# The last layer's middle down projection as seven block products, with the order of its instructions written out

## The chip, the cores and the metric

The kernel runs on one core of a Trainium2 chip. The metric is the device time of one execution in microseconds. Before the change three runs took 1272.74, 1273.72 and 1275.20 us, the median being 1273.72 us.

The engines that matter are TensorE (PE: matmuls and transposes, with PEld for its weight loads), VectorE (DVE), ScalarE (ACT), GpSimd (POOL) and SyncE (SP). SP only issues DMA transfers, and POOL's queue issues those that accumulate into their destination. Each engine runs its own instructions in a fixed order and waits on semaphores for the others.

## What is computed

The reference is a trunk of two decoder layers on 512 tokens of width 1024. Each layer has a mixer (sparse attention, gated linear attention and spatial gating) and then a feed-forward part:

```python
for l in range(DEPTH):                       # DEPTH = 2
    ...
    x = x + jnp.concatenate([o_nsa, o_gla, o_sg], axis=-1) @ w_out[l]
    h = rmsnorm(x, ffn_norm[l])
    x = x + (jax.nn.silu(h @ w_gate[l]) * (h @ w_up[l])) @ w_down[l]
return rmsnorm(x, final_norm)
```

`w_gate` and `w_up` have 1024 rows and D_FF = 2816 columns (22 tiles of 128); `w_down` is 2816 x 1024. The change concerns `@ w_down[l]` in the last layer, for 8 of the 22 tiles of its inner dimension. Everything is float32.

## The kernel before

**Precision.** An operand is kept as two tiles, `hi` (rounded to the type that TensorE takes) and `lo` (the rest). `mm3` (L384) issues three matmuls for each product: hi x hi, hi x lo, lo x hi. For weights, `w_split` (L363) makes the pair from a loaded tile `raw` of 128 x 1024: ScalarE writes `hi` (L367) and VectorE subtracts (L370). For operands, `split_psum` (L347) does the same (L348, L349). The pairs of weights live in four buffers `hl`, so that a split waits until the matmuls that used the buffer two products earlier are done. Loaded weights live in three buffers `raw`, two `wx` and two `wy`.

**The feed-forward part** (`ffn`, L1457) cuts the 22 tiles of D_FF into two halves of 11 and works in three blocks (`PARTS`): tiles 0 to 2, 3 to 6 and 7 to 10 of each half. The middle block, the one that matters here, so has 8 tiles: 4 of half 0 and 4 of half 1.

Gate and up projections of the second and third block are done by `quads` (L1519), a form of Strassen's product. It takes the operands as 2 x 2 blocks (two halves of the inner dimension, two halves of the tokens or columns) and does seven block products in place of eight, in the order 1, 2, 5, 6, 7, 3, 4. Each block product is 2 token tiles x 4 inner tiles x 3 = 24 matmuls of 512 columns. The operand sums are made ahead (`Ops`, L557). The weight sums are made in `wx` and `raw`: `summed` loads one block with SP and then adds another with a transfer that accumulates, issued on POOL's queue (L1526); for products 6 and 4, VectorE adds a block that was loaded into another buffer (L1585, L1612). The sums of results form in the PSUM banks A, B and C (two banks each), and VectorE and ScalarE take them out (`copy`, `use`).

**The down projection of a block** follows its gate and up projections. `turned` (L1654) transposes the block's result `zb` (tokens on partitions; in the last layer `zb` is the buffer `xT`) into PSUM, 16 transposes for each half, and splits it into operand tiles `act`. `down_tok` (L1381) then multiplies plainly: for each of 2 column halves, 2 pairs of token tiles, 8 inner tiles and 2 tiles of a pair, one `mm3`, which is 192 matmuls; VectorE adds the results to the residual `xt` (L1402).

In the loop over blocks (L1689) the middle block of the last layer runs as follows: gate products, up products, transposes of half 1, gate product 1 of the third block, transposes of half 0, gate product 2 of the third block, `down_tok`, and then the rest of the third block. `finish` ends the kernel.

**The order of the work.** A scheduler orders each engine's instructions by priority (`tc.high_priority`). In one part of the kernel the order is written out: `in_order` (L618) takes the instructions that were traced since `mark[0]`, numbers them for each engine from 0 in the order of tracing, leaves out the DMA transfers, and chains them in the order of the table `ORDER`. Around the middle block's down projection there is no such table before the change.

Of the kernel before, what the change touches and what calls it, by code (L numbers as in the profile page):

```python
# [19 lines left out]
P = 128  # L20
# [16 lines left out]
WPRI = 400  # L37
WU = (5, 2, 1)
EPRI = 600
EP = {}  # L40
JS = 3
XPOOL = (1,)
# [61 lines left out]
    "Pool": (  # L104
        "0-2 11 20 4 3 5-6 9 7-8 10 13 19 12 14 16 15 17 38 29 18 22 21 23-24 26 25 27 47 28 33 31 30 32 56 34 36 35 37 "
        "39-42 44 46 43 45 51 49 48 50 52 55 54 53 58 57 60 59 64 61-63 65 68 66-67 71 70 72 69 73-79 "
    ),
}
LEVELS = (64, 32, 16, 8, 4, 2, 1)
# [81 lines left out]
def trunk_kernel(ctx: ExitStack, tc: tile.TileContext, a, out):  # L191
# [192 lines left out]
    def mm3(ps, lh, ll, rh, rl, start, stop, skip=False):  # L384
        nc.tensor.matmul(ps, lh, rh, start=start, stop=False, skip_group_check=skip)  # L385
        nc.tensor.matmul(ps, lh, rl, start=False, stop=False, skip_group_check=skip)  # L386
        return nc.tensor.matmul(ps, ll, rh, start=False, stop=stop, skip_group_check=skip)  # L387
# [227 lines left out]

    mark = [None]

    def in_order():  # L618
        traced = nc.cur_bb.bb.instructions
        k0 = next(k for k in reversed(range(len(traced))) if traced[k] is mark[0]) + 1  # L620
        for engine, runs in ORDER.items():
            work = [i for i in traced[k0:] if i.engine == getattr(mybir.EngineType, engine)
                    and not isinstance(i, mybir.InstDMACopy)]
            runs = [[int(n) for n in r.split("-")] for r in runs.split()]
            line = [work[n] for r in runs for n in range(r[0], r[-1] + 1)]
            assert len(set(i.name for i in line)) == len(work)
# [830 lines left out]
    def ffn(l, fp, norm, kts, ops, kts_next, nrm_next, g_next):  # L1457
# [19 lines left out]
        def plain_block(fl):  # L1477

            acts, rb = [], None
            steps = [5, 6, 7, 0]  # L1480

            def through(pss):
                gx, th, ux = t_(), t_(), t_()
                nc.vector.tensor_tensor(gx, pss[0], rb, op=ALU.mult)  # L1484
                nc.scalar.activation(th, gx, AF.Tanh, scale=0.5)
                nc.vector.scalar_tensor_tensor(ux, pss[1], 0.5, rb, op0=ALU.mult, op1=ALU.mult)
                nc.vector.tensor_tensor(ux, ux, gx, op=ALU.mult)
                nc.vector.scalar_tensor_tensor(ux, th, 1.0, ux, op0=ALU.add, op1=ALU.mult)
                act = fp.tile([P, 2, SEQ], F32R, tag="act", name=nm("act"), bufs=8)
                split_psum(act[:, 0, :], act[:, 1, :], ux)  # L1490
                acts.append(act)
            for n, f in enumerate(fl):
                pss, us = [], []
                for mat, tag in (("w_gate", "g"), ("w_up", "s")):
                    u = w_rows(a[mat][l], 0, 8, f * P, P)
                    pss.append(psum(tag))
                    us.append(u)

                ks = [(b, k) for k_ in ((range(6), (6, 7)) if n == 0 else (range(KT),)) for b in range(2) for k in k_]
                if n == 1:  # L1500
                    ks.insert(KT, None)
                for bk in ks:
                    if bk is None:
                        in_order()
                        rb = begin()
                        through(*held)
                        continue
                    b, k = bk
                    x_ = kts[k // 2]
                    ins = mm3(pss[b], us[b][:, 0, k, :], us[b][:, 1, k, :], x_[:, k % 2, 0, :], x_[:, k % 2, 1, :], k == 0, k == KT - 1)  # L1510
                if n:
                    through(pss)
                else:
                    held = [pss]
                if n and steps:
                    ops.need(steps.pop(0))
            return acts

        def quads(mat, c0, w, copy, use, pri=WPRI):  # L1519

            def rows(k0, half, u):
                return a[mat][l][(k0 + 2 * u) * P : (k0 + 2 * u + 2) * P, half * HF + c0 : half * HF + c0 + w].rearrange(
                    "(k p) c -> p k c", p=P)

            def load(dst, k0, half, u, q=None):
                (q or nc.sync).dma_start(dst[:, 0 : 2 * w].rearrange("p (k c) -> p k c", k=2), rows(k0, half, u),  # L1526
# [28 lines left out]
            def product(i, us, ps, start, stop):  # L1555
                for tt in range(2):
                    tk = slice(tt * P, (tt + 1) * P)
                    for kt in range(4):
                        u = us[kt // 2][:, :, kt % 2, :]
                        mm3(ps[tt][:, 0:w], ops.at(i, kt, 0)[:, tk], ops.at(i, kt, 1)[:, tk], u[:, 0], u[:, 1],  # L1560
                            start and kt == 0, stop and kt == 3, True)

            A = [psum("g") for _ in range(2)]

            product(1, plain(0, 0), A, True, True)
            yield
            B = [psum("s") for _ in range(2)]
            product(2, plain(4, 0), B, True, True)
            yield
            with tc.high_priority(offset=EPRI):  # L1570
                c11 = [copy(tt, 0, A[tt][:, 0:w]) for tt in range(2)]
                for tt in range(2):
                    use(tt, 0, c11[tt], B[tt][:, 0:w])
            C = [psum(x) for x in "so"]

            X, us = summed(0, 0, 0, 1, "wx")
            product(5, us, C, True, True)
# [3 lines left out]
            for u in range(2):  # L1581
                raw = raw_("wy", 2)
                load(raw, 4, 1, u)
                with tc.high_priority(offset=pri):
                    nc.vector.tensor_tensor(X[u][:, 0 : 2 * w], X[u][:, 0 : 2 * w], raw[:, 0 : 2 * w], op=ALU.add)  # L1585
                Y.append(raw)
                us.append(view(w_split(2 * w, X[u], pri)))
            product(6, us, A, False, True)
# [17 lines left out]

            us = []
            for u in range(2):
                raw = raw_("raw", 3)
                load(raw, 4, 0, u)  # L1610
                with tc.high_priority(offset=pri):
                    nc.vector.tensor_tensor(X[u][:, 0 : 2 * w], X[u][:, 0 : 2 * w], raw[:, 0 : 2 * w], op=ALU.add)  # L1612
# [41 lines left out]
        def turned(n, half):  # L1654
# [8 lines left out]
                res.append(act)  # L1663
            return res

        def down_m(fl, acts, m, nb, w, last=True, early=False):
# [22 lines left out]
        for n, (f0, nb) in enumerate(parts):  # L1689
# [3 lines left out]
            if n == 0:  # L1693
                acts = plain_block(fl)
                if xt is not None:
                    token_major(xt)
                ops.need(3)
            else:
                list(todo[n][0])
                list(todo[n][1])  # L1700
                after = last_cast[0]
# [66 lines left out]
```

## Time and profile before

The profiled execution is a fourth one, with its own time.

| | |
|---|---|
| median of three runs | 1273.72 us (1272.74 to 1275.20) |
| profiled execution | 1269.01 us |
| its span, first to last instruction | 1267.2 us |
| mean granted TensorE clock | 0.998 |
| TensorE busy | 1245.8 us (98%) |
| VectorE busy | 900.2 us (71%) |
| ScalarE busy | 662.5 us (52%) |
| middle block, last layer: up products | 1050.0 to 1088.1 us of the span |
| transposes and two gate products of the third block | 1088.1 to 1102.5 us |
| `down_tok` of the middle block | 1102.5 to 1146.0 us |

Times are counted from the start of the span. A row of the timeline has the start in us, the duration in us, the engine, the line of the kernel and the operation; `[0.56 <-ACT act L348]` behind it says how long the engine was idle just before and what ended the idle time. A row of the groups has line, engine, operation, out<-in with shapes and a count, then busy us and the mean ns of one, then the idle time before them with its releasers. A row of the windows has, for one stretch, each engine's busy time and number of instructions, then the granted clock, the mean busy share of the 16 DMA engines and GB/s. Matmuls are pipelined, so their durations overlap; what one costs is read from start to start.

### The profile page before, as it was taken

The numbers are of one execution on the slowest core, as the hardware profiler recorded it, in microseconds if no ns is written. First come the engines' busy times: TensorE is split into PE (matmuls) and PEld (weight loads), VectorE is DVE, ScalarE is ACT, GpSimd is POOL, SyncE is SP. The second block draws the span as 40 slices with busy tenths as digits, with TensorE's granted clock in tenths as the row PEclk, the third lists the DMA queues.
The fourth block names the chain that finished last, engine by engine and source line by source line (L and its number), as shares of the span: only waits on it lengthen the run. The fifth ranks groups of instructions, "written<-read, shape, count | busy, mean of one in ns | idle before, by whom it ended". The sixth has DMA issues, their size and how long they took to land.

```text
span 1267.2 us, 18084 instructions
## 1 busy us (share of the span) xinstructions
PE 1245.8 (98%) x6678; PEld 1036.3 (82%) x6678; DVE 900.2 (71%) x1549; ACT 662.5 (52%) x1256; POOL 205.3 (16%) x253
## 2 busy tenths in 40 slices
PE   8999999999999999999999999999999999999997
PEld 7887778888888888888888877788888888888886
DVE  6767789967856874587446667998776467727775
ACT  6675358865433552354346733778554345515532
POOL 0101224532000100010301002345300001000002
PEclk9999999999999999999999999999999999999999
DMA  6461350053335885483434316301433548744811
GB/s 234 132 194 34 98 128 18 19 132 117 96 107 147 197 244 131 110 212 90 114 94 152 117 34 142 97 21 48 121 115 100 132 125 228 203 110 143 222 67 67
DMA packets 134204, 155.02 MB, mean 122 GB/s; under 512 B 9306, under 2 KB 86884, under 8 KB 134116
## 3 DMA queue, kind: packets, MB, share of 16 engines
q1 hardware_dynamic: 117392, 128.81, 33.4%
q0 software_dynamic: 10208, 20.84, 9.4%
q10 hardware_dynamic: 6516, 4.22, 1.4%
q8 instruction: 52, 0.85, 0.3%
q14 instruction: 36, 0.29, 0.1%
HBM read 149.92 MB, written 2.10 MB: 120 GB/s over the span
## 4 chain that ended last, share of the span: by engine, by line
PE 85%; DVE 6%; ACT 4%; issue 2%; DMA 2%; ACTq 0%
PE banks L385 23%; PE banks L386 22%; PE banks L387 22%; PE banks L1319 3%; PE banks L1337 2%; PE banks L1336 2%; DMA raw<-in_w_in_dram 1%; ACT hl L367 1%; PE banks L1300 1%; PE banks L1301 1%; PE banks L1660 1%; PE banks L520 1%; PE banks L1033 1%; DVE hl L370 1%; DVE w1h L807 1%
## 5 line engine op out<-in xcount | busy, mean ns | idle before, releaser
L367 ACT CAST hl<-raw 128x1024 fp32r<-128x1024 f32 (+3 forms) x170 | 175.3, 1035 | 213.7 <-PE banks L387 163.4
L370 DVE TENSOR_TENSOR hl<-raw,hl 128x1024 fp32r<-128x1024 f32 (+3 forms) x170 | 204.4, 1207 | 85.5 <-ACT hl L367 84.1
L385 PE MATMUL banks<-hl,kt 128*128 128x512 f32 (+2 forms) x688 | 259.3, 377 | 1.5 <-ACT hl L367 1.4
L387 PE MATMUL banks<-hl,kt 128*128 128x512 f32 (+2 forms) x688 | 257.7, 375 | 0.0
L386 PE MATMUL banks<-hl,kt 128*128 128x512 f32 (+2 forms) x688 | 256.7, 373 | 0.0
L386 PE MATMUL banks<-kt,hl 128*128 128x512 f32 x384 | 150.1, 393 | 0.0
L385 PE MATMUL banks<-kt,hl 128*128 128x512 f32 x384 | 150.0, 398 | 0.0
L385 PEld LDWEIGHTS banks<-hl,kt 128*128 128x128 f32 x688 | 129.6, 188 | 24.6 <-ACT hl L367 2.0
L387 PE MATMUL banks<-kt,hl 128*128 128x512 f32 x384 | 149.7, 393 | 0.0
L387 PEld LDWEIGHTS banks<-hl,kt 128*128 128x128 f32 x688 | 129.8, 189 | 21.3
L386 PEld LDWEIGHTS banks<-hl,kt 128*128 128x128 f32 x688 | 129.5, 188 | 21.2
L1312 POOL TENSOR_SCALAR P<-P,rc,gates 128x384 f32<-128x384 f32 (+3 forms) x128 | 77.6, 620 | 92.5 <-DVE rc L1310 81.2
L367 ACT CAST hl<-wx 128x1024 fp32r<-128x1024 f32 x48 | 50.5, 1052 | 78.8 <-PE banks L387 72.4
L387 PEld LDWEIGHTS banks<-kt,hl 128*128 128x128 f32 x384 | 72.3, 188 | 13.7
L385 PEld LDWEIGHTS banks<-kt,hl 128*128 128x128 f32 x384 | 71.9, 188 | 14.2 <-DVE ft L1484 0.4
L386 PEld LDWEIGHTS banks<-kt,hl 128*128 128x128 f32 x384 | 72.3, 188 | 13.0
L549 DVE TENSOR_TENSOR xT<-xT,banks 128x512 f32<-128x512 f32 x56 | 37.6, 682 | 50.3 <-PE banks L387 50.1
L370 DVE TENSOR_TENSOR hl<-wx,hl 128x1024 fp32r<-128x1024 f32 x48 | 58.7, 1223 | 19.9 <-ACT hl L367 19.3
L386 PE MATMUL banks<-act,hl 128*128 128x512 f32 x172 | 67.1, 390 | 0.0
L387 PE MATMUL banks<-act,hl 128*128 128x512 f32 x172 | 67.0, 389 | 0.0
L385 PE MATMUL banks<-act,hl 128*128 128x512 f32 x172 | 66.9, 390 | 0.0
L386 PE MATMUL banks<-hl,act 128*128 128x512 f32 (+1 forms) x164 | 63.0, 384 | 0.0
(357 smaller groups left out, 2392.2 us busy)
## 6 DMA issues: line engine op xcount, KB each, us to landing
raw<-in_w_gate_dram SPq DMA_DIRECT2D x44, 512.0 KB, 3.7
raw<-in_w_up_dram SPq DMA_DIRECT2D x44, 512.0 KB, 4.3
raw<-in_w_in_dram SPq DMA_DIRECT2D x32, 512.0 KB, 3.6
raw<-in_w_down_dram SPq DMA_DIRECT2D x36, 256.0 KB, 4.0
raw<-in_w_down_dram SPq DMA_DIRECT2D x18, 512.0 KB, 3.6
raw<-in_w_out_dram SPq DMA_DIRECT2D x16, 512.0 KB, 3.4
raw<-in_cmp_w_k_dram SPq DMA_DIRECT2D x8, 512.0 KB, 3.8
raw<-in_cmp_w_v_dram SPq DMA_DIRECT2D x8, 512.0 KB, 4.4
```

The costliest lines, as they stand in the source:

```text
L367: last_cast[:] = [nc.scalar.copy(hl[:, 0, 0:n], raw[:, 0:n])]
L370: e_.tensor_tensor(hl[:, 1, 0:n], raw[:, 0:n], hl[:, 0, 0:n].bitcast(F32), op=ALU.subtract)
L385: nc.tensor.matmul(ps, lh, rh, start=start, stop=False, skip_group_check=skip)
L386: nc.tensor.matmul(ps, lh, rl, start=False, stop=False, skip_group_check=skip)
L387: return nc.tensor.matmul(ps, ll, rh, start=False, stop=stop, skip_group_check=skip)
L520: ins = nc.tensor.matmul(pw[t], xkt[n][:, kk, p, t * P : t * P + P], eu[n][0][:, q, kk, :], start=n == 0 and p + q + kk == 0, stop=n == 3 ...
L549: nc.vector.tensor_tensor(xT[:, m, :], xT[:, m, :], ps, op=ALU.add)
L807: nc.vector.tensor_tensor(hl[:, 1], raw[:, q * 512 : q * 512 + 512], hl[:, 0].bitcast(F32), op=ALU.subtract)
L1312: nc.gpsimd.tensor_scalar(ps_[i], ps_[i], rc[:, i : i + 1], gates[:, i, 3 * h + 1 + br : 3 * h + 2 + br], op0=ALU.mult, op1=ALU.mult)
L1319: nc.tensor.transpose(T[:, c : c + P], ps_[i][:, j * P : (j + 1) * P], ident)
L1336: nc.tensor.matmul(O[:, j * P : SEQ], lhs, pt[:, 0, c : c + n], start=first, stop=False)
L1337: nc.tensor.matmul(O[:, j * P : SEQ], lhs, pt[:, 1, c : c + n], start=False, stop=h > 0 and br == 1 and j == 0)
```

## The change

The last layer's middle down projection is done by `quads` too. The operands come from the transposes: `DownOps.turned(1)` transposes half 1, splits its first 256 tokens and copies all of it back to `zb`; `turned(0)` transposes half 0, splits all of it, and `sums` makes the differences and sums for products 5, 6 and 3 from the PSUM banks and the copy. `split(6)`, `split(7)` and `split(3)` make the remaining operand pairs between the products. Some of them overwrite operand tiles whose product is done. With `far=True`, `quads` adds weights for products 6 and 4 by accumulating transfers on POOL's queue and not on VectorE. Each result bank is added to the residual or subtracted from it (`add`), 14 times in place of 8.

Gate product 1 of the third block stays between the two sets of transposes; its gate product 2 now comes after the down products. The new table `ORDER_DOWN` chains 392 instructions of TensorE, 102 of VectorE and 64 of ScalarE, traced from the start of the middle block's up products to the end of its down products.

In the table's numbers, TensorE's 0 to 167 are the up products (24 each, in the order 1, 2, 5, 6, 7, 3, 4), 168 to 183 the transposes of half 1, 184 to 207 gate product 1 of the third block, 208 to 223 the transposes of half 0, and 224 to 391 the seven down products in the same order: 224 is product 1, 248 product 2, 272 product 5, 296 product 6, 320 product 7, 344 product 3, 368 product 4. Within a product the first 12 belong to the first token tile. VectorE's 30 and 31 are the last of up, 32 to 35 the splits of half 1, 38 to 41 those of half 0, 42 to 53 the sums, 54 to 57 the splits for product 5, and from 58 on the down products' weight splits (58, 59 for product 1; 64, 65 for 2; 78, 79 for 5; 84, 85 for 6; 88, 89 for 7; 94, 95 for 3; 98, 99 for 4), operand splits and additions (74 to 77, 86, 87, 90 to 93, 96, 97, 100, 101).

The core of the diff:

```diff
+OPRI = 260
...
+ORDER_DOWN = {
+    "PE": (
+        "0-1 24 2 36 3 25-27 37 28 4-5 12-15 6 16 7 38-39 8 17-21 9 40 22 48 10 41 60 29 11 61 42 49 23 30 62-64 50 "
...
+        "127-129 146-147 130 135 148 136 131 137-138 212 139-141 149-150 168 142-143 172 158-159 151 160-161 180 "
+        "152-155 181 176 216 169 162-163 182 173 170 164 184 177 174 171 165 178 217 166-167 183 175 185 179 218 213 "
+        "186-188 196-197 189-191 198 192 219 199 208 214 209 215 210-211 200 224 193 236 225 237 201 238 194 202 195 "
+        "203 226 239 204-205 220 227 221 206-207 240-242 228-229 243 230 244-245 231 222 248 232-235 246-247 249 260 "
+        "223 272 250 273 261-263 274 264-265 275 266 276 251 277-278 252-256 284 257 285 279 286 267-268 287 269-270 "
+        "288-290 258 271 259 291 280-281 296 282 292 308 297 309-310 298 311-313 299-301 293 314 294 302-304 315 "
+        "305-307 316-317 283 295 318-329 332 330 333-336 331 337-347 368 348-349 369 350 370-372 351 373 380 374 "
+        "381-382 356-357 383 358-361 352-353 375 384 362-363 354 376 364 385 365 377 366-367 355 386-391 378-379 "
+    ),
+    "DVE": (
+        "0 2 1 8 3 10 9 11-13 26 6 14-15 7 4 20-21 5 16 27 18 28 19 17 29 22-25 36 30 37 32 31 35 34 33 58-59 38-40 42 "
+        "45 48 46-47 43-44 64 49 78 50 54 65 79 55 41 56 51-53 61 66 68 75 62 70 72 60 74 63 67 84 80 69 57 73 77 85 81 "
+        "88 71 86 89 87 94 83 95 90-91 98-99 92-93 76 82 97 96 101 100 "
+    ),
+    "Activation": (
...
-    def in_order():
+    def in_order(table):
...
-        for engine, runs in ORDER.items():
+        for engine, runs in table.items():
...
-                        in_order()
+                        in_order(ORDER)
...
-        def quads(mat, c0, w, copy, use, pri=WPRI):
+        def quads(mat, c0, w, copy, use, pri=WPRI, rows=None, at=None, tags=("gg", "ss", "so"), far=False):
...
+            def grow(x, raw, half, u):
+                if far:
+                    load(x, 4, half, u, nc.gpsimd)
+                    return
+                with tc.high_priority(offset=pri):
+                    nc.vector.tensor_tensor(x[:, 0 : 2 * w], x[:, 0 : 2 * w], raw[:, 0 : 2 * w], op=ALU.add)
...
+        class DownOps:
...
+            def turned(self, half):
+                pss = []
+                for b in range(4):
+                    ps = psum(("osss", "tsto")[half][b])
+                    for t in range(NT):
+                        nc.tensor.transpose(ps[:, t * P : (t + 1) * P], zb[:, 2 * t + half, b * P : (b + 1) * P], ident)
+                    pss.append(ps)
+                for b, ps in enumerate(pss):
+                    act = fp.tile([P, 2, SEQ], F32R, tag="act", name=nm("act"), bufs=8)
+                    (self.k1 if half else self.k2).append(act)
+                    if half:
+                        split_psum(act[:, 0, 0:256], act[:, 1, 0:256], ps[:, 0:256])
+                        nc.scalar.copy(zb[:, 2 * b + 1, :], ps)
+                    else:
+                        split_psum(act[:, 0, :], act[:, 1, :], ps)
+                if not half:
+                    self.sums(pss)
...
+            def sums(self, pss):
+                tt, stt = nc.vector.tensor_tensor, nc.vector.scalar_tensor_tensor
+                s5 = []
+                for b, ps in enumerate(pss):
+                    a11, a21, s6, s3 = self.parts(b)
+                    z = t_()[:, 0:256]
+                    tt(z, ps[:, 256:512], a21, op=ALU.subtract)
+                    stt(s6, z, -1.0, a11, op0=ALU.mult, op1=ALU.subtract)
+                    stt(s3, s6, -1.0, ps[:, 0:256], op0=ALU.mult, op1=ALU.subtract)
+                    s5.append(z)
+                with tc.high_priority(offset=OPRI):
+                    for b, z in enumerate(s5):
+                        split_psum(self.at(5, b, 0), self.at(5, b, 1), z)
...
+            def add(self, t, half, *parts):
+                y = xt[:, t, half * 512 : (half + 1) * 512]
+                nc.vector.tensor_tensor(y, y, parts[-1], op=ALU.subtract if half else ALU.add)
+
+            def products(self):
+                return quads("w_down", 0, 512, self.add, self.add, rows=self.rows, at=self.at, tags=("tt", "os", "ss"), far=True)
...
                 list(todo[n][0])
+                if xt is not None and not last:
+                    mark[0] = nc.cur_bb.bb.instructions[-1]
                 list(todo[n][1])
+                if xt is not None and not last:
+                    down = DownOps(f0)
+                    down.turned(1)
+                    next(todo[n + 1][0])
+                    with tc.high_priority(offset=WPRI - OPRI):
+                        down.turned(0)
+                    g = down.products()
+                    next(g)
+                    with tc.high_priority(offset=OPRI):
+                        down.split(6)
...
+                    list(g)
+                    in_order(ORDER_DOWN)
+                    continue
```

More of the change, by code (lines that the diff above doesn't have):

```diff
@@ L106 @@
         "39-42 44 46 43 45 51 49 48 50 52 55 54 53 58 57 60 59 64 61-63 65 68 66-67 71 70 72 69 73-79 "
+    ),
+}
+ORDER_DOWN = {
[12 rows of a table added]
+    ),
+    "DVE": (
[3 rows of a table added]
+    ),
+    "Activation": (
+        "0-3 6 4 7-8 5 9 12-13 10 16 11 17 14 18 15 19 28-29 20 38 22 24 26 21 27 39 25 30 23 31-32 44 34-35 45 50 40 "
+        "36 51 42 41 33 47 37 52-53 46 43 56 49 55 57 48 54 58-63 "
     ),
@@ L1517, in plain_block, with gate_rows @@
             return acts
-        def quads(mat, c0, w, copy, use, pri=WPRI):
-            def rows(k0, half, u):
+        def quads(mat, c0, w, copy, use, pri=WPRI, rows=None, at=None, tags=("gg", "ss", "so"), far=False):
+            def gate_rows(k0, half, u):
                 return a[mat][l][(k0 + 2 * u) * P : (k0 + 2 * u + 2) * P, half * HF + c0 : half * HF + c0 + w].rearrange(
                     "(k p) c -> p k c", p=P)
+            rows, at = rows or gate_rows, at or ops.at
             def load(dst, k0, half, u, q=None):
@@ L1559, in product @@
                         u = us[kt // 2][:, :, kt % 2, :]
-                        mm3(ps[tt][:, 0:w], ops.at(i, kt, 0)[:, tk], ops.at(i, kt, 1)[:, tk], u[:, 0], u[:, 1],
+                        mm3(ps[tt][:, 0:w], at(i, kt, 0)[:, tk], at(i, kt, 1)[:, tk], u[:, 0], u[:, 1],
                             start and kt == 0, stop and kt == 3, True)
-            A = [psum("g") for _ in range(2)]
+            def grow(x, raw, half, u):
[4 more added lines that the diff above has]
+                    nc.vector.tensor_tensor(x[:, 0 : 2 * w], x[:, 0 : 2 * w], raw[:, 0 : 2 * w], op=ALU.add)
+            A = [psum(x) for x in tags[0]]
             product(1, plain(0, 0), A, True, True)
             yield
-            B = [psum("s") for _ in range(2)]
+            B = [psum(x) for x in tags[1]]
             product(2, plain(4, 0), B, True, True)
@@ L1573, in quads @@
                     use(tt, 0, c11[tt], B[tt][:, 0:w])
-            C = [psum(x) for x in "so"]
+            C = [psum(x) for x in tags[2]]
             X, us = summed(0, 0, 0, 1, "wx")
@@ L1583, in quads @@
                 load(raw, 4, 1, u)
-                with tc.high_priority(offset=pri):
-                    nc.vector.tensor_tensor(X[u][:, 0 : 2 * w], X[u][:, 0 : 2 * w], raw[:, 0 : 2 * w], op=ALU.add)
+                grow(X[u], raw, 1, u)
                 Y.append(raw)
@@ L1608, in quads @@
             for u in range(2):
[L1609 to L1612, printed above, removed]
+                raw = raw_("raw", 3) if not far else None
+                if not far:
+                    load(raw, 4, 0, u)
+                grow(X[u], raw, 0, u)
                 us.append(view(w_split(2 * w, X[u], pri)))
@@ L1664, in turned, with __init__, at, rows @@
             return res
+        class DownOps:
+            def __init__(self, f0):
+                self.f0 = f0
+                self.k1, self.k2 = [], []
+                self.op5 = fp.tile([P, 4, 2, 256], F32R, name=nm("op5"))
+            def at(self, i, kt, s_):
+                if i == 5:
+                    return self.op5[:, kt, s_, :]
+                c = 256 if i in (4, 7) else 0
+                return (self.k1 if i in (1, 6, 7) else self.k2)[kt][:, s_, c : c + 256]
+            def rows(self, k0, half, u):
+                r0 = (self.f0 + 2 * u + (0 if k0 else NF // 2)) * P
+                return a["w_down"][l][r0 : r0 + 2 * P, half * 512 : (half + 1) * 512].rearrange("(k p) c -> p k c", p=P)
+            def turned(self, half):
[15 more added lines that the diff above has]
+                    self.sums(pss)
+            def parts(self, b):
+                return [zb[:, 2 * b + h, c : c + 256] for h in (1, 0) for c in (0, 256)]
+            def sums(self, pss):
[11 more added lines that the diff above has]
+                        split_psum(self.at(5, b, 0), self.at(5, b, 1), z)
+            def split(self, i):
+                for b in range(4):
+                    a11, a21, s6, s3 = self.parts(b)
+                    if i == 7:
+                        s3 = t_()[:, 0:256]
+                        nc.vector.tensor_tensor(s3, a11, a21, op=ALU.subtract)
+                    split_psum(self.at(i, b, 0), self.at(i, b, 1), s6 if i == 6 else s3)
+            def add(self, t, half, *parts):
[3 more added lines that the diff above has]
+                return quads("w_down", 0, 512, self.add, self.add, rows=self.rows, at=self.at, tags=("tt", "os", "ss"), far=True)
@@ L1699, in ffn @@
                 list(todo[n][0])
+                if xt is not None and not last:
+                    mark[0] = nc.cur_bb.bb.instructions[-1]
                 list(todo[n][1])
+                if xt is not None and not last:
[8 more added lines that the diff above has]
+                        down.split(6)
+                    next(g)
+                    with tc.high_priority(offset=OPRI):
+                        down.split(7)
+                    next(g)
+                    with tc.high_priority(offset=OPRI):
+                        down.split(3)
+                    list(g)
+                    in_order(ORDER_DOWN)
+                    continue
                 after = last_cast[0]
```

2 rows, old and new, of the table ORDER_DOWN are left out of this document.

## The prediction

> **What bounds the kernel now.** I read the page's engine shares, then the windows around the change, then TensorE's timeline.
>
> ```profile
> span 1267.2 us, 18084 instructions
> ...
> PE 1245.8 (98%) x6678; PEld 1036.3 (82%) x6678; DVE 900.2 (71%) x1549; ACT 662.5 (52%) x1256; POOL 205.3 (16%) x253
> ```
>
> ```profile
> core 0: us, PE busy (x) PEld busy (x) DVE busy (x) ACT busy (x) POOL busy (x), PEclk, DMA share, GB/s
> 1050.00:1088.10 38.10, 38.10 (x169) 31.51 (x169) 30.65 (x33) 18.65 (x21) 4.81 (x4) 1.00 0.86 223
> 1088.10:1102.50 14.40, 14.40 (x81) 12.45 (x80) 11.24 (x15) 9.02 (x15) 0.00 (x0) 1.00 0.84 249
> 1102.50:1146.00 43.50, 43.50 (x193) 36.02 (x193) 18.68 (x21) 9.72 (x10) 2.41 (x2) 1.00 0.39 97
> ```
>
> The rows are the middle block's up products, then its transposes beside the first two gate products of the next block, then its down projection. TensorE is busy in every microsecond of all three, at full clock (column PEclk). So a matmul taken out here shortens the kernel, and there is no idle time that a new order could win: the list can only lose. The third row is the one that changes: VectorE has 24.8 us to spare in it, and DMA runs at 0.39.
>
> **The matmuls removed.** The plain product has 8 operand tiles x 4 token tiles x 2 column halves x 3 = 192 matmuls. Seven block products have 7 x 2 x 4 x 3 = 168. All are of the same shape.
>
> ```profile
> 1102.55 0.39 PE L385 MATMUL banks<-hl,act 128*128 128x512 f32 x1
> ...
> 1146.07 0.39 PE L385 MATMUL banks<-hl,kt 128*128 128x512 f32 x1
> ```
>
> These are the first start of the plain product and the first start behind it: 43.52 us for 192, so 0.2267 us each (0.39 is the pipelined length). 24 fewer are 5.44 us less. The Trainium skill ("TensorE: Matmul & The Clock Gate", Part 1) gives N / 2.4 GHz + 2.5 ns from start to start at full clock. For 512 columns that is 0.2157 us, an estimate by which the saving would be 5.18 us; the trace's cadence decides.
>
> **The transposes.** Their number stays 32. Before they stand in two blocks of 16; in the list they stand in 16 groups among matmuls.
>
> ```profile
> 1088.14 1.91 PE L1660 MATMUL banks<-ident,xT 128*128 128x128 f32 x16
> 1089.80 0.48 PE L385 MATMUL banks<-hl,kt 128*128 128x512 f32 x1
> 1090.12 0.40 PE L386 MATMUL banks<-hl,kt 128*128 128x512 f32 x1
> ```
>
> ```profile
> 822.08 0.39 PE L1348 MATMUL banks<-pcT,vcb 128*128 128x512 f32 x1
> 822.31 0.27 PE L1319 MATMUL banks<-ident,P 128*128 128x128 f32 x1
> 822.34 0.47 PE L386 MATMUL banks<-kt,hl 128*128 128x512 f32 x1
> 822.65 0.39 PE L387 MATMUL banks<-kt,hl 128*128 128x512 f32 x1
> ```
>
> A block of 16 costs 1.66 us and a first gap that is 0.32 instead of 0.23, so 0.110 each. A lone one between 512-column matmuls costs 822.65 - 822.08 - 2 x 0.2267 = 0.117. For 32 that is 0.2 us more.
>
> **What VectorE and ScalarE get.** The prices:
>
> ```profile
> L370 DVE TENSOR_TENSOR hl<-raw,hl 128x1024 fp32r<-128x1024 f32 x10 | 12.2, 1224 | 9.1 <-ACT hl L367 9.1
> L367 ACT CAST hl<-raw 128x1024 fp32r<-128x1024 f32 x10 | 10.4, 1050 | 22.6 <-PE banks L387 20.1 <-DMA raw<-in_w_gate_dram 1.7 <-DMA raw<-in_w_down_dram 0.8
> L349 DVE TENSOR_TENSOR act<-banks,act 128x512 fp32r<-128x512 f32 x8 | 5.0, 682 | 0.0
> L1402 DVE TENSOR_TENSOR zb<-zb,banks 128x512 f32<-128x512 f32 x7 | 4.8, 685 | 15.1 <-PE banks L387 15.1
> ```
>
> ```profile
> 1063.79 1.22 DVE L370 TENSOR_TENSOR hl<-wx,hl 128x1024 fp32r<-128x1024 f32 x1
> 1064.92 1.22 DVE L1612 TENSOR_TENSOR wx<-wx,raw 128x1024 f32<-128x1024 f32 x1
> ...
> 1083.76 0.68 DVE L1648 TENSOR_TENSOR ft<-ft,banks 128x512 f32<-128x512 f32 x1
> 1084.36 1.22 DVE L370 TENSOR_TENSOR hl<-raw,hl 128x1024 fp32r<-128x1024 f32 x1
> ```
>
> ```profile
> 972.23 1.43 DVE L584 SCALAR_TENSOR_TENSOR kt<-sg,kt 128x256 fp32r<-128x256 f32 x4
> ```
>
> Back to back, an operation of 1024 columns takes 1.13 us of VectorE, one of 512 takes 0.60, and one of 256 takes (1.43 - 0.08) / 4 = 0.34, where 0.08 is the overlap that the starts above show (0.68 against 0.60). Before, the down part has 8 weight splits, 8 operand splits of 512 and 8 additions: 8 x (1.13 + 0.60 + 0.60) = 18.6 us. After, it has 14 weight splits, 14 additions of 512, 4 operand splits of 512 and 36 operations of 256 (4 splits of half 1, 12 sums, 12 splits for products 5, 6, 3, and 8 for product 7): 15.8 + 8.4 + 2.4 + 12.2 = 38.8 us. VectorE gets 20 us more, in 38.1 us of products and about 9 us of transposes and gate product ahead of them. It just fits, without much to hide a mistake in the order. ScalarE's work in the stretch (14 weight casts of 1.05 and 28 shorter ones) stays below VectorE's.
>
> **What moves.** Gate product 2 of the next block goes from ahead of the down products to behind them, with its two loads on SP's queue, its splits, and the evacuations that follow it. It then stands as in the middle block, whose gate products ran so:
>
> ```profile
> 984.00:1022.00 38.00, 38.00 (x170) 31.46 (x169) 18.75 (x21) 10.92 (x12) 2.39 (x2) 1.00 0.46 111
> ```
>
> No gap, so I cost the move at nothing; the down products 3 and 4 cover its loads and splits (its weight buffers come free 23 and 8 matmuls before the list's end, 5.2 and 1.8 us, against 2.4 needed, and the second is used 6 matmuls later). The up products are only interleaved anew; the walk below finds no wait among them.
>
> **Where the list makes TensorE wait.** I laid the three lists side by side with these prices and looked for matmuls with too few others between them and what they need. When a matmul frees a weight buffer, the drain (0.39 - 0.23 = 0.16), the cast (1.05) and the subtraction (1.22) follow, 2.43 us, before the second matmul on the new weights.
>
> - Matmul 295, the last of product 5, frees the buffer that 327 in product 7 needs. Nine matmuls lie between, 2.04 us: a wait of 0.4, with the slow restart 0.5.
> - From 295 to 344 (product 3, which needs the bank that addition 91 frees) lie 26 matmuls, 5.9 us, and the wait above. VectorE has after 295 the chain of 2.4 us and then 87, 94, 83, 95, 90, 91, that is 0.60 + 1.13 + 0.34 + 1.13 + 0.60 + 0.68 = 4.5. A wait of 0.5.
> - From the end of the up products (167) to 284 (product 5, whose bank the last of the sums, 53, frees) lie 70 matmuls and 16 transposes, 17.6 us. VectorE has 25 operations from 58 to 53: 6 x 1.13 + 4 x 0.60 + 15 x 0.34 = 14.3, from about 2.0 behind 167 (operations 31, 35, 34, 33 stand first), with 0.7 of waiting for transposes that the list puts late and about 1.0 where sums follow each other through their results. That is 18.0, so 0.5 with the restart.
>
> Together 1.5 us. They are bounded by 0 (each rests on a few tenths, and a VectorE that is 3% quicker closes two) and by twice as much.
>
> **The two DMA chains.** Products 5, 6, 7 and 4 get their weights' sums by accumulating transfers on Pool's queue; 6 and 4 used VectorE for it in the gate blocks. The buffer wx is read by the split for 5, then written by the transfer, then split for 6.
>
> ```profile
> L1526 SPq DMA_DIRECT2D wx<-in_w_gate_dram x8: 367/368/411, 260.8 to 1080.3; - x8
> ...
> DMA to landing us min/median/max: 3.5/3.8/4.9
> ```
>
> ```profile
> L1526 POOL DMA_DIRECT2D wx<-in_w_gate_dram x8: 1194/1203/1642, 267.1 to 1085.4; - x8
> ...
> DMA to landing us min/median/max: 5.8/8.3/9.8
> ```
>
> The first answer is wx's plain loads, the second its accumulating ones. Matmul 229 frees the buffer for product 5's first split; from there to 296, the first of product 6, lie 53 matmuls and 2 transposes, 12.2 us. The chain needs 2.4, half a microsecond of VectorE's queue, the transfer and one cast of 1.05: 4.0 + 8.3 = 12.3 at the median. The waits above push 296 back by 0.5, so at 8.3 nothing is lost, and from 8.7 on each microsecond costs one.
>
> The second chain is new behind the change: wx is held until product 4's split, and the next gate block's product 5 needs it 78 matmuls after 337 (54 of the list and 24 of gate product 2), 17.7 us. Drain, cast, VectorE's queue (2.0), subtraction, issue (0.37), load (3.8), accumulation (8.3) and cast make 17.9, the second buffer about 1 us later with 1.4 of matmuls in between. A wait of 0.2 at the median, 1.3 at 9.8. Before, the last of these transfers started at 1080.3 and 1085.4 (the rows above), far ahead.
>
> The Trainium skill ("DMA: Bandwidth & Descriptors", the anatomy of a SWDGE transfer) fits 2.0 us + bytes / 436e3 for a transfer from GpSimd. For 512 KB that is 3.2 us, an estimate. By it both chains close 5 us early and their 0.2 us goes. The landings of 5.8 to 9.8 in this trace speak against it.
>
> **The sum.** -5.44 + 0.2 + 1.5 + 0.2 = -3.5, and half a microsecond more for restarts and for Pool's and SP's queues, whose order the list leaves out: -3.0 us. The profiled execution took 1269.01 us (span 1267.2), 4.7 below the median of the three runs, 1273.72; the difference applies to either. Forecast 1273.72 - 3.0 = **1270.7 us**. A measurement of this kernel tells 0.2%, 2.5 us, from no change.
>
> **The rivals.**
>
> *All waits hidden.* VectorE's sums come out a little quicker, transfers land at their median: -5.44 + 0.2 + 0.5 = -4.7, 1269.0 us. For it: the three waits are tenths. Against: with 38.8 us of work in some 47, VectorE can't make up a late start.
>
> *The accumulating transfers land at the top of their spread, 9.8 us.* Then 296 waits 1.1, the gate product 1.3, each with a restart and a second wait for the subtraction of about 0.3, on top of 1.5 + 0.2: a loss of 4.7, so -0.7, 1273.0 us. For it: the down stage moves 14 loads of 512 KB and 4 more for the accumulations into X in 38 us, 9.4 MB or 248 GB/s, the rate of the second window, where the DMA engines are at 0.84. Against: the up stage ran at 223 GB/s and 0.86 without one wait on TensorE.
>
> *The transfers saturate: slower than before.* The same two chains with landings of 12 us. 296 waits 3.3, the gate product 3.5, product 4 (its chain has 3 us of slack) 1.3, and 2 us of restarts and the small waits: a loss of 10, so +4.6, 1278.3 us. It decides from a landing of about 10 us on and passes +2.5 at 11. For it: 18 transfers where the plain product had 8. Against: none of the 16 accumulating wx transfers took over 9.8.
>
> **Chances.** Forecast 0.38, all hidden 0.16, top of the spread 0.34, saturated 0.12. The first two are faster by over 0.2%, the third is within, the last slower. The range goes from all hidden, less 1 us for the runs' own scatter (1272.74 to 1275.2), to the third case plus 2.5: 1268.0 to 1275.5. It leaves out the saturated case and little else.
>
> **What would show it.** Right: 168 matmuls in the down part at 0.227 us; TensorE's gaps of 0.3 to 0.7 us at product 5's second token tile, product 7's third operand and product 3's start, put down to VectorE; VectorE busy over 85% from the first sum to product 3. Wrong: gaps over 1 us ahead of product 6 or of the next block's gate product 5, put down to ScalarE behind a DMA (second and third rival); landings of wx over 9.8; a cadence other than 0.227; or new waits at the end of the kernel, which I take as unchanged.

## The result and the profile after

The change made the kernel slower. Seven executions took 1277.15 to 1280.83 us, median 1279.07, against 1268.60 to 1275.20, median 1271.04, for seven of the kernel before: a ratio of 1.0062, with a 95% interval of 1.005 to 1.0074. The forecast was 3.0 us faster, with a range from 5.7 us faster to 1.8 us slower. The loss is 8.0 us.

The profiled execution took 1278.19 us. The engines' row of its page and the windows around the change (us from:to and length, busy time and number of instructions of each engine, granted clock, DMA share, GB/s) are these. Lines of the kernel carry higher numbers than before: L385 is now L410, L367 is L392, L370 is L395, and a load (L1526) is L1553.

```profile
PE 1246.7 (98%) x6654; PEld 1031.9 (81%) x6654; DVE 920.1 (72%) x1593; ACT 674.8 (53%) x1282; POOL 215.6 (17%) x261
```

```profile
core 0: us, PE busy (x) PEld busy (x) DVE busy (x) ACT busy (x) POOL busy (x), PEclk, DMA share, GB/s
...
1102.50:1141.00 38.50, 34.58 (x145) 26.11 (x144) 29.54 (x48) 17.78 (x29) 8.48 (x7) 1.00 0.92 204
...
1147.90:1151.20 3.30, 0.25 (x2) 0.05 (x1) 0.07 (x1) 1.04 (x1) 0.00 (x0) 1.00 1.11 201
1151.20:1156.00 4.80, 4.04 (x9) 2.60 (x10) 4.03 (x5) 1.67 (x2) 0.00 (x0) 0.65 0.77 140
```

24 matmuls fewer, and yet TensorE's total has not fallen: 1246.7 us against 1245.8. A part of the reason is that matmuls at the lower clock are busy for longer (0.63 us instead of 0.39, in the rows below). In the first of these windows, the down part, it stands still for 3.9 of 38.5 us; from 1147.9 to 1151.2 it does next to nothing; and after that it runs at a granted clock of 0.65. Before, it was busy throughout, at 1.00. The share of the DMA engines went from 0.39 to 0.92 while the rate only went from 97 to 204 GB/s.

The waits of TensorE between 1090 and 1180 us, grouped (total, times, longest), say who was late. There was not one such row before.

```profile
PE banks L410 <- ACT hl L392: 5.9, 3, 3.0
PE banks L411 <- DVE hl L395: 1.6, 3, 0.8
PE banks L410 <- DVE xT L1745: 0.7, 2, 0.5
```

The last row is the forecast's wait of product 5 for the sums. The first two are the split of weights, the cast and then the subtraction. TensorE's timeline shows where: at product 6 of the down projection (1116.37) and at product 5 of the third block's gate (1151.15), where it restarts slowly.

```profile
1114.16 0.39 PE L410 MATMUL banks<-hl,op 128*128 128x512 f32 x1
1116.37 0.50 PE L410 MATMUL banks<-hl,act 128*128 128x512 f32 x1 [1.82 <-ACT hl L392]
...
1147.72 0.39 PE L412 MATMUL banks<-hl,kt 128*128 128x512 f32 x1
1151.15 0.50 PE L410 MATMUL banks<-hl,kt 128*128 128x512 f32 x1 [3.05 <-ACT hl L392]
1152.41 0.62 PE L411 MATMUL banks<-hl,kt 128*128 128x512 f32 x1 [0.76 <-DVE hl L395]
1152.83 0.63 PE L412 MATMUL banks<-hl,kt 128*128 128x512 f32 x1
...
1156.02 0.42 PE L410 MATMUL banks<-hl,kt 128*128 128x512 f32 x1
```

From 1152.41 to 1156.02 the matmuls start 0.42 us apart and more, where the rest of the stage has 0.227: eight steps take 3.61 us in place of 1.81.

The cast was itself waiting. Between 1107 and 1153 us the chain that ended last goes through three transfers: the second accumulation for product 6, the load into the first buffer of the gate's product 5, and the accumulation into its second buffer (the one into the first was issued at 1142.36):

```profile
1107.74 12.59 DMA wx<-in_w_down_dram
...
1132.52 9.21 DMA wx<-in_w_gate_dram
1141.80 0.54 issue
...
1143.61 8.93 DMA wx<-in_w_gate_dram
```

And POOL's queue shows in which order the accumulations were issued: `raw` is product 7's, `wx` is product 6's.

```profile
1102.72 1.20 POOL L1553 DMA_DIRECT2D raw<-in_w_down_dram  x1 [11.74 <-DVE xT L1744]
1104.79 1.20 POOL L1553 DMA_DIRECT2D wx<-in_w_down_dram  x1 [0.87 <-DVE xT L1745]
1106.64 1.22 POOL L1553 DMA_DIRECT2D raw<-in_w_down_dram  x1 [0.65 <-issue]
1107.74 1.38 POOL L1553 DMA_DIRECT2D wx<-in_w_down_dram  x1
```

Product 7 comes after product 6, but its accumulations go ahead of product 6's and between them, so that four are in flight at once. Product 6's land 10.4 us (1104.79 to the cast's start at 1115.27) and 12.6 us after their issue; the forecast took 8.3.

### The profile page after: what moved, and what is told of

Its sections match the earlier page's. It is cut to its first block, busy times and chain, and to the rows that moved or that the text cites. A ratio compares the mean times of both kernels' runs of the same rounds, so it can differ in the third digit from the quotient of the medians.

```text
span 1276.4 us, 18142 instructions
## 1 busy us (share of the span) xinstructions
PE 1246.7 (98%) x6654; PEld 1031.9 (81%) x6654; DVE 920.1 (72%) x1593; ACT 674.8 (53%) x1282; POOL 215.6 (17%) x261
## 4 chain that ended last, share of the span: by engine, by line
PE 78%; DVE 7%; DMA 5%; ACT 5%; issue 3%; ACTq 0%; POOL 0%; POOLq 0%; DVEq 0%
PE banks L410 21%; PE banks L411 20%; PE banks L412 20%; PE banks L1344 3%; PE banks L1362 2%; ACT hl L392 2%; PE banks L1361 2%; DVE hl L395 2%; DMA wx<-in_w_gate_dram 1%; DMA raw<-in_w_in_dram 1%; DMA raw<-in_w_down_dram 1%; PE banks L1325 1%; DMA wx<-in_w_down_dram 1%; PE banks L545 1%; PE banks L1326 1%
## 5 line engine op out<-in xcount | busy, mean ns | idle before, releaser
L392 ACT CAST hl<-raw 128x1024 fp32r<-128x1024 f32 (+3 forms) x168 | 173.0, 1034 | 193.5 <-PE banks L412 146.4
L410 PE MATMUL banks<-hl,kt 128*128 128x512 f32 (+2 forms) x688 | 259.1, 378 | 4.5 <-ACT hl L392 4.2
L395 DVE TENSOR_TENSOR hl<-raw,hl 128x1024 fp32r<-128x1024 f32 (+3 forms) x168 | 201.9, 1206 | 74.8 <-ACT hl L392 73.6
L410 PEld LDWEIGHTS banks<-hl,kt 128*128 128x128 f32 x688 | 130.0, 189 | 28.4 <-ACT hl L392 5.4
L410 PE MATMUL banks<-kt,hl 128*128 128x512 f32 x384 | 149.9, 398 | 0.0
L392 ACT CAST hl<-wx 128x1024 fp32r<-128x1024 f32 x54 | 56.8, 1051 | 89.4 <-PE banks L412 59.6
L395 DVE TENSOR_TENSOR hl<-wx,hl 128x1024 fp32r<-128x1024 f32 x54 | 66.0, 1223 | 34.6 <-ACT hl L392 34.3
L410 PEld LDWEIGHTS banks<-kt,hl 128*128 128x128 f32 x384 | 71.9, 188 | 14.1 <-DVE ft L1509 0.4
L410 PE MATMUL banks<-act,hl 128*128 128x512 f32 x172 | 66.8, 390 | 0.0
L374 DVE TENSOR_TENSOR PT<-banks,PT 128x384 fp32r<-128x384 f32 (+1 forms) x96 | 55.7, 593 | 8.5 <-ACT PT L373 8.0
```

The lines of the kernel that those rows point to most:

```text
L374: nc.vector.tensor_tensor(lo, src, hi.bitcast(F32), op=ALU.subtract)
L392: last_cast[:] = [nc.scalar.copy(hl[:, 0, 0:n], raw[:, 0:n])]
L395: e_.tensor_tensor(hl[:, 1, 0:n], raw[:, 0:n], hl[:, 0, 0:n].bitcast(F32), op=ALU.subtract)
```

## The experiments

Theory A says that the loss sits in the two transfer chains: product 6's, made late by the order on POOL's queue, and the gate product 5's, which starts only when product 4 lets `wx` go; a clock drop follows the second. Rival B says that the transfers are simply too many for the DMA engines. Rival C blames the written-out list. Eight kernels were run, in two groups (e1 to e4, e5 to e8), each group beside the kernel before on the same chip. What one kernel gains on the change, or on a kernel of the other group, is a difference of two such ratios, and uncertain by some 2 us.

| kernel | ratio to the kernel before | interval |
|---|---|---|
| the change | 1.0062 | 1.0050 to 1.0074 |
| e1: own buffers for the gate's product 5 | 1.0026 | 1.0015 to 1.0037 |
| e2: product 7's accumulations behind 6's | 1.0025 | 1.0014 to 1.0037 |
| e3: both | 1.0003 | 0.9995 to 1.0012 |
| e4: no list | 1.0100 | 1.0085 to 1.0116 |
| e5: e3, with the up transfers behind the gate's | 0.9989 | 0.9979 to 1.0000 |
| e6: 16 more matmuls in the gap | 1.0052 | 1.0040 to 1.0065 |
| e7: product 7's accumulations left out | 1.0021 | 1.0012 to 1.0031 |
| e8: kernel before, 24 matmuls left out | 0.9958 | 0.9946 to 0.9970 |

**e8, the matmuls by themselves.** In the kernel before, `down_tok` skips one of its eight operand tiles:

```diff
+                    if len(acts) < 8 or k != 3:
                         mm3(ps[b], acts[k][:, 0, tk], ...
```

> The kernel before with 24 of the 192 matmuls of the middle block's down projection left out (three of every 24, one operand tile of eight) and nothing else changed, so that the product is not complete. It measures the term on which the forecast rests, by itself: 24 x 0.2267 = 5.4 us less, a ratio of 0.9957. A rival by which the time of a matmul taken out here comes back as a wait later (for the third block's weights, or at the end) gives 0.998 to 1.000.

The ratio is 0.9958, 5.3 us of 1271. The first start of the plain product and the first start behind it, in the kernel with 168 matmuls:

```profile
1103.56 0.39 PE L385 MATMUL banks<-hl,act 128*128 128x512 f32 x1
...
1141.64 0.39 PE L385 MATMUL banks<-hl,kt 128*128 128x512 f32 x1
```

That is 38.08 us, 0.2267 each, and 5.44 less than the 43.52 of before. The saving is real and nothing takes it back, as long as nothing else changes. So whatever the change lost came with what it added.

**e4, no list.**

```diff
-                    in_order(ORDER_DOWN)
```

> The changed kernel with the list of the down stage taken out, so that the engines keep the order in which the program was scheduled; the seven products and the summed operands stay. Theory A (the loss comes from the transfer chains, not from the list's order): the transposes and the sums now stand in blocks that TensorE has to wait for, the transfer waits stay, so slower than the changed kernel by 3 us or more (1.009 or above). Rival C (the list is at fault: it puts small waits on a VectorE without room and pulls the weights' chain late): as fast as the changed kernel or faster, 1.003 to 1.006.

1.0100, so the list is worth 0.4% and rival C falls. The longest waits of TensorE from 1085 to 1180 us without it:

```profile
PE banks L410 <- ACT hl L392: 5.1, 2, 4.0
PE banks L410 <- DVE xT L1745: 2.9, 2, 2.0
PE banks L1721 <- ACT xT L1728: 1.5, 1, 1.5
```

The waits for the weights' split stay (5.1 against 5.9), and waits for the sums and for transposes' banks come on top. Part of the 0.4% is the clock: behind waits of 2.04 and 3.99 us this kernel runs at half cadence (last section). The list does its work; it does not reach the transfers.

**e2, the order on POOL's queue.** An edge puts product 7's accumulations behind the last one that product 6 needs:

```diff
-                    load(x, 4, half, u, nc.gpsimd)
+                    grown[:] = [load(x, 4, half, u, nc.gpsimd)]
...
-                    load(raw, k1, half1, u, nc.gpsimd)
+                    with tc.issue_after(grown[0].ins) if grown else ExitStack():
+                        load(raw, k1, half1, u, nc.gpsimd)
```

> The changed kernel, but on Pool's queue the accumulations for product 7 are issued behind the two for product 6 instead of ahead of them and between them. Theory A (the order on the queue, which the list leaves out, makes product 6 late): wx lands about 8 us after its issue instead of 10.4 and 12.6, the gaps of 2.0 + 1.2 + 0.5 us at product 6 fall below 1 in all, and product 7 has enough cover to take its transfers later: 2 to 3 us less than the changed kernel, a ratio to the kernel before of 1.004. Rival B (four accumulations share the DMA engines, the order does not matter): product 6 gains 1 us at most and product 7 gives it back, no difference to the changed kernel (1.006). The gate product's wait stays by both.

1.0025, 4.7 us less than the change, more than the 2 to 3 expected. POOL's queue, the landing of its `wx` transfers from 1080 to 1170 us, and TensorE's two longest waits:

```profile
1104.02 1.20 POOL L1554 DMA_DIRECT2D wx<-in_w_down_dram  x1 [13.49 <-DVE xT L1747]
1106.96 1.20 POOL L1554 DMA_DIRECT2D wx<-in_w_down_dram  x1 [1.74 <-DVE op L374]
1107.80 2.87 POOL L1554 DMA_DIRECT2D raw<-in_w_down_dram  x2
```

```profile
DMA to landing us min/median/max: 5.9/7.5/9.4
```

```profile
PE banks L410 <- ACT hl L392: 2.8, 1, 2.8
PE banks L411 <- DVE hl L395: 0.6, 1, 0.6
```

No `wx` transfer of this stretch takes over 9.4 us now (12.6 in the change), both waits at product 6 are gone, and what is left in these rows is the gate's. I had left some of product 6's wait standing; all of it went.

**e7, the contention without the order.** The change, but `summed` makes no accumulating transfer for the down projection's product 7:

```diff
-                    load(raw, k1, half1, u, nc.gpsimd)
+                    if not (far and tag == "raw"):
+                        load(raw, k1, half1, u, nc.gpsimd)
```

> The changed kernel without product 7's two accumulating transfers in the down projection (its weights are then one block instead of a difference of two, so the product is another one); all else as in the changed kernel. Theory A (the order on Pool's queue is what made product 6 late): no better than the kernel that only puts them behind product 6's, 1.0025 within 0.001. Rival B (their share of the DMA engines counts whatever the order): product 6's and then the gate's accumulations land 1 to 2 us earlier still, and the ratio falls below 1.001.

1.0021, which can't be told from e2. Taking the two transfers away gives no more than putting them behind. So for product 6 the order decides: the same two transfers, issued behind product 6's, cost nothing that can be told here.

**e1, own buffers for the gate's product 5.** The space of the down projection's operands for product 5 (`op5`) is free after that product. It becomes two tiles, and the gate's weight sums for its product 5 use them:

```diff
-                    raw = raw_(tag, 2)
-                    load(raw, k0, half, u)
+                    own = lent and tag == "wx" and (mat, c0) == ("w_gate", 7 * P)
+                    raw = raw_("op5" if own else tag, 2)
+                    first = load(raw, k0, half, u)
...
```

> The changed kernel, but the third block's gate product 5 gets its two weight-sum buffers from the space of product 5's operands (free once the down projection's product 5 has run), and no longer waits for wx, which is held until the down projection's product 4. Theory A (most of the loss is this second transfer chain: in the changed kernel TensorE stands 3.2 + 1.0 + 0.7 us ahead of and in gate product 5, and runs at a granted clock of 0.65 for 4.8 us after it, worth 1.9): these gaps and the clock drop go, 6.8 us less, so about 1.5 us above the kernel before (1.0011). Rival B (the transfers are too many for the DMA engines, whatever buffer they go to): the loads that now go earlier land late all the same or push others back, under 2 us less, a ratio of 1.005 or more. The waits at product 6 (2.0 + 1.2 + 0.5) stay by both.

1.0026, 4.6 us less than the change, not 6.8. The gap, its second wait and the slow cadence are gone, but a new row, the second, has come:

```profile
PE banks L410 <- ACT hl L392: 2.3, 2, 1.3
PE banks L410 <- ACT xT L1664: 1.1, 1, 1.1
```

The first row is product 6 of the down projection. The second is the gate's product 7, which waits for the copy that takes product 6 out of its bank.

**e3, both.**

> Both edits, the own buffers for the third block's gate product 5 and product 7's accumulations behind product 6's. Theory A with both causes: 6.8 + 2 to 3 us less than the changed kernel, 1.0 to 2.0 us faster than the kernel before (0.9985 to 0.9992). Rival B: no faster than the changed kernel by more than 2 us (1.0045 or more).

1.0003: 7.5 us of the 8.0 come back. The interval holds neither rival B's 1.0045 nor any of theory A's 0.9985 to 0.9992. The two gains nearly add up: 4.6 + 4.7 would be 9.3, and with each of them uncertain by some 2 us it is not shown whether anything is missing. The row of e1 is still there, and this kernel's trace explains it. ScalarE and POOL, ahead of that copy:

```profile
1154.73 1.05 ACT L392 CAST hl<-raw 128x1024 fp32r<-128x1024 f32 x1 [5.16 <-DMA raw<-in_w_gate_dram]
1155.68 0.58 ACT L1666 COPY xT<-banks 128x512 f32<-128x512 f32 x1
```

```profile
1143.60 1.23 POOL L1554 DMA_DIRECT2D wx<-in_w_up_dram  x1 [8.24 <-DVE hl L395]
...
1146.35 1.30 POOL L1554 DMA_DIRECT2D raw<-in_w_gate_dram  x1
```

The same fault one step on. The up projection, whose product 5 is some 40 us away, now finds `wx` free early; its accumulations stand ahead of the gate's on POOL's queue. The gate's cast waits 5.16 us for its weights, and the copy that TensorE needs is queued behind that cast on ScalarE, though its own input is ready.

**e5, the up transfers behind the gate's.** e3, and two edges more, on SP's queue and on POOL's:

```diff
+                    up = lent and tag == "wx" and (mat, c0) == ("w_up", 7 * P)
+                    with tc.issue_after(lent[-2].ins) if up else ExitStack():
...
+                    with tc.issue_after((grown[0] if grown else lent[-1]).ins) if grown or up else ExitStack():
```

> The kernel with own buffers and product 7's accumulations behind product 6's, and beside that the third block's up projection comes later on both queues: its two weight-sum loads behind the gate product 7's loads on SP's queue, its accumulations behind the gate product 7's on Pool's. Theory A (order on the queues): in the kernel without this, the up loads took 14.2 us to land among the gate's, and the gate product 7's second accumulation stood behind them on Pool's queue, landed 8.3 us later, held ScalarE's queue and with it the copies on which TensorE waited 1.2 + 0.3 us; these go, so about 1.5 us less than the kernel without it and 1 to 1.5 us less than the kernel before, a ratio of 0.9988 to 0.9992. Rival B (too many transfers): the wait moves to another product of the gate or up part, and the ratio stays at 1.000 or above.

0.9989, inside the expected 0.9988 to 0.9992. This version is clearly faster than the change. Against the kernel before its interval ends at 1.0000, so a gain of 0.1% stands at the edge of what can be told, and the interval overlaps that of e3. The mechanism is read from TensorE's waits from 1085 to 1180 us, all of them:

```profile
PE banks L410 <- DVE xT L1677: 0.9, 2, 0.5
PE banks L410 <- DVE zb L1773: 0.9, 2, 0.5
PE banks L410 <- DVE xT L1755: 0.6, 2, 0.4
```

No transfer is left among them, and no ScalarE. What remains is VectorE six times, at products 5, 3 and 4 of the down projection (second and third row) and twice at the gate (first row).

**e6, the clock.** The change, with 16 matmuls in the gap ahead of the gate's product 5, whose results are overwritten:

```diff
...
+            if mat == "w_gate" and xt is not None and c0 == 7 * P:
+                for _ in range(16):
+                    nc.tensor.matmul(C[0][:, 0:w], at(2, 0, 0)[:, 0:P], held2[0][1][:, 0, 1], start=True, stop=True)
```

> The changed kernel with 16 matmuls of 512 columns more on TensorE ahead of the third block's gate product 5, in the gap of 3.2 us; what they write is overwritten by product 5. They take 16 x 0.227 = 3.6 us, 0.4 more than the gap. Theory A (the granted clock of 0.65 behind that gap comes from the gap itself): the clock stays at 1.00, product 5's first matmuls run at 0.227 us instead of 0.43, 1.9 us less, and with the 0.4 the kernel is 1.5 us faster than the changed one, a ratio to the kernel before of 1.005. Rival (the slow cadence has another cause, such as the weights' splits or the transfers): the first matmuls of product 5 stay at 0.42 us, and the kernel is 0.4 us slower than the changed one or the same.

The ratio, 1.0052, is near the expected one, but its interval overlaps the change's, so the time decides nothing. The timeline and the window of product 5:

```profile
1147.19 3.79 PE L1612 MATMUL banks<-hl,kt 128*128 128x512 f32 x16
1150.82 0.39 PE L410 MATMUL banks<-hl,kt 128*128 128x512 f32 x1
1151.05 0.39 PE L411 MATMUL banks<-hl,kt 128*128 128x512 f32 x1
```

```profile
1151.00:1157.00 6.00, 5.45 (x24) 4.18 (x24) 5.08 (x6) 3.46 (x5) 0.00 (x0) 1.00 0.26 48
```

Product 5 starts at 0.23 us a matmul and at a clock of 1.00, with the same weights and splits, where the change had 0.42 us and 0.65. The transfers are not the same in time: the cast of product 5's first weights begins at 1146.35 here, ahead of the 16 matmuls, and at 1150.06 in the change, and behind it the share of the DMA engines is 0.26 in place of 0.77. That leaves the transfers as a rival; e2 rules it out, whose slow matmuls ran with no transfer in flight (last section). So the slow cadence was the gap's doing. What it costs in time is not shown by this run: the gate's products 5 and 6 now wait 0.55, 1.00 and 0.73 us for subtractions.

## Why the prediction was wrong

**The matmuls.** -5.44 us: right, and shown by itself in e8.

**The transposes.** Their 0.2 us can't be seen beside the waits; nothing rests on it.

**The small waits for VectorE.** 1.5 us, between 0 and 3. In the change product 5's wait shows as 0.7 us idle (the wait for L1745 above), and those at products 7 and 3 lie behind the late product 6. Where product 6 is on time (e5), the down projection's VectorE waits are 0.9 + 0.6 = 1.5 us idle, at products 5, 3 and 4 instead of 5, 7 and 3. Right in total, and partly by luck: the wait at product 7 did not come, and one at product 4 that the forecast did not have took its place.

**The two DMA chains.** This is the step that failed. The forecast took 8.3 us for an accumulating transfer and 3.8 for a load, the medians of the kernel before, and so 0.2 us for both chains.

- Chain one, product 6: 10.4 and 12.6 us instead of 8.3, so TensorE starts 2.0 and 1.2 us late, and 0.7 more goes to the subtractions that follow. 3.9 us where the forecast had none. The cause is the order on POOL's queue (e2, e7). The forecast put POOL's and SP's order, which the list leaves out, at half a microsecond together with all restarts.
- Chain two, the gate's product 5: the load took 9.2 us instead of 3.8, with 0.6 to the issue of the accumulation and 7.7 until its landing (1142.36 to the cast at 1150.06). That is 17.5 where 12.5 stood. So the accumulation kept to the forecast and the load did not. Idle 3.2 us, the second wait 1.0, and 0.7 at a later matmul. That the chain can begin only when product 4 frees `wx` is what makes it late: with buffers of their own (e1) the wait is gone. Why the load itself took 9.2 us is open; it ran among two loads of `wy` and an accumulation at a share of 0.94 (1128 to 1142 us). The size also differs between executions: in e6, with the same instructions up to there, the chain took 14.6 us (1131.80 to 1146.35) and not 17.5.
- The clock, not priced at all: 3.61 - 1.81 = 1.8 us for the eight slow steps.

Together 3.9 + 3.2 + 1.0 + 0.7 + 1.8 = 10.6 us, with product 5's 0.9 and restarts of 0.1 each (0.34 us from the first start behind a wait to the next, where 0.23 is usual) some 12.3. Less the 5.44 saved that is about 7, and the runs show 8.0; the last microsecond is not placed.

**The rivals.** The third described what came, in kind: it put product 6's wait at 3.3 and the gate's at 3.5 from landings of 12 us. It had the chance 0.12. Its loss was 4.6 us against 8.0 measured. That its time of 1278.3 lies near the measured 1279.07 is luck, as the kernel before took 1271.04 in these runs and not 1273.72. And the gate's wait came from a slow load, not from the accumulation. What was argued against it, that no `wx` transfer of the kernel before took over 9.8 us, was the wrong evidence: there, no more than two accumulations were issued within 5 us of each other, here four. Its name was half wrong as well, since with the right order the same transfers fit (e3, e5).

**What the profile of before held.** The forecast compared rates, 248 GB/s against 223 in the up stage. But bytes of the two kinds don't cost the same. The DMA queues of the kernel before, between 1050 and 1088 us (packets, MB, share of the 16 engines):

```profile
q1 hardware_dynamic: 3171, 6.10, 49.3%
q0 software_dynamic: 1216, 2.34, 36.5%
```

Plain loads: 6.10 MB in 49.3% of 38 us, 326 GB/s. Accumulating transfers: 2.34 MB in 36.5%, 169 GB/s, half as fast. By these rates (an estimate) a load of 512 KB holds the engines for 1.6 us and an accumulation for 3.1. Four accumulations and a load that start within 5 us need 14 us of them. The change between 1104 and 1119 us:

```profile
q0 software_dynamic: 1068, 2.07, 83.8%
q1 hardware_dynamic: 477, 0.91, 18.8%
```

The engines are full (the shares add up to over 100), and the rates are the same, 165 and 323 GB/s. An estimate from these rows, with the accumulations in the order of issue on POOL's queue, could have been made ahead of the run.

## What to carry to other kernels

A list that orders the compute engines does not order the queues that feed them: walk SP's and POOL's queues as well, and put an edge where a transfer that is needed later may go first. Price a transfer by the time that it holds the DMA engines, each kind by its own row, and add up those in flight together; a landing measured with two in flight says little about four. And when a step saves little, look at what it holds longer: here a buffer kept for three more products cost a wait one block on, and the idle time cost the clock.

## What the runs showed of the hardware

- A gap lowers the clock of what follows it. Behind 3.05 us of idle TensorE, one matmul and 0.76 us more, the change ran eight matmuls at 0.42 us and more. e2 did so behind 2.81 and 0.58 us, and its slow matmuls ran with no transfer in flight (share 0.00) that could be to blame. The first two rows are e2's gap and what followed. The others are from e4, where a single gap of 2.04 us was enough:

```profile
1144.70:1147.50 2.80, 0.00 (x0) 0.00 (x0) 0.02 (x1) 1.09 (x2) 0.00 (x0) 1.00 1.08 195
1148.80:1154.40 5.60, 5.60 (x13) 4.44 (x14) 5.52 (x7) 3.21 (x4) 0.00 (x0) 0.50 0.00 0
```

```profile
1108.96 0.39 PE L412 MATMUL banks<-hl,act 128*128 128x512 f32 x1
1111.38 0.72 PE L410 MATMUL banks<-hl,act 128*128 128x512 f32 x1 [2.04 <-DVE xT L1745]
1111.89 0.63 PE L411 MATMUL banks<-hl,act 128*128 128x512 f32 x1
1112.32 0.63 PE L412 MATMUL banks<-hl,act 128*128 128x512 f32 x1
```

  Gaps of 1.8 us (product 6) and 1.1 us (e3) left it at full cadence. The Trainium skill ("TensorE: Matmul & The Clock Gate", Part 1) gives 426.7 ns from start to start at half clock for 512 columns, and an idle window of about 3.4 us after which the clock falls. The cadence agrees (0.42 us from 1152.41 to 1152.83); here 2.04 us of idle time was enough.
- An accumulating transfer holds the DMA engines about twice as long as a plain load of the same size (169 against 326 GB/s), and of 512 KB it landed after 5.7 to 12.6 us in these runs, by what else was in flight.
